# The first block of a row-sum kernel loaded as two partition halves from two issuing engines

## The chip, the core and the metric

The kernel runs on one core of a Trainium2 chip. A core has several engines that work side by side and meet only through semaphores. Those that matter here are VectorE (DVE in the profile), ScalarE (ACT), GpSimd (POOL) and SyncE (SP; its instructions that issue transfers are listed as SPq). Sixteen DMA engines move data between the chip's memory (HBM) and the core's working memory (SBUF), which has 128 partitions. The metric is the device time of one execution in microseconds; less is better.

## The reference

The input is 32 × 512 rows of 1024 float32 numbers, 67.1 MB. The output is one float32 for each row: the sum of its positive entries.

```python
def setup_inputs():
    batch, seq, dim = 32, 512, 1024
    return {"x": np.random.randn(batch, seq, dim).astype(np.float32)}

def reference(x: np.ndarray) -> np.ndarray:
    relu_x = np.maximum(x, 0)
    return np.sum(relu_x, axis=-1).astype(np.float32)
```

There is one clamp and one addition for each number read, and 64 KB of output.

## The kernel before

The 16,384 rows are taken as eight blocks of 2,048 rows. A block is 128 partitions × 16 rows × 1024 numbers: 64 KB in each partition and 8.39 MB in all. The first block is the first 2,048 rows of the input, 16 neighbouring rows to a partition (`xf`, line 83); the others are cut from the rest of the input (`xv`, line 84). Three SBUF buffers `io0` to `io2` of one block each are used in turn (line 74).

The loop of lines 183 to 203 goes over seven blocks. For each, SyncE issues one transfer for the whole block (the helper `load`, lines 101 to 108; the issue is line 103 in the profile). Each load has a semaphore of its own, which the transfer raises by 16 when it has landed. From the fourth block on, the load first waits until VectorE has finished with the block that was in its buffer three blocks ago (`freed`, lines 104, 105 and 185). SyncE does nothing but issue transfers and wait, in program order.

The work on a block is split by `TWO` (line 14): ScalarE clamps a run of rows in place (`clamp`, activation in line 144), and VectorE sums the clamped run (`total`, tensor_reduce in line 152). The first two blocks are one run of 16 rows each, the next ones two runs of 8. Some rows at the end are done whole by one engine, clamp and sum in one instruction: ScalarE in line 159 and VectorE in line 167. Before its first clamp ScalarE loads its table of functions (line 142), and that instruction carries the wait for the first block.

The eighth block is cut into loads that become smaller (lines 206 to 244: 8 rows, 4 rows, and four pieces of the last 4 rows), so that little work is left when the last bytes land. GpSimd clamps one small piece (line 234), VectorE folds the last piece in (line 254), and SyncE stores the sums in three transfers (line 115).

The order on the queues is written out by hand; nothing is planned by a tool. `open_without_barrier` (lines 268 to 284) edits the program's opening: it takes out the barrier and moves the first load (`EARLY = 1`) ahead of everything else that SyncE does, so that the first load is SyncE's first instruction. At the end, `tile_relu_sum_kernel` clears the semaphores (lines 47 to 50). All transfers are issued by SyncE, on one queue.

## Time and profile before

| what | value |
|---|---|
| device time, median of 3 runs | 161.03 us (160.95 to 161.07) |
| span of the profiled execution, first to last instruction | 159.7 us |
| the profiled execution's own time | its span is all that the profile gives; the median of the runs is 1.3 us above it |
| DVE busy | 118.8 us (74% of the span) |
| ACT busy | 103.6 us (65%) |
| DMA moved | 67.18 MB, mean 421 GB/s, 98.0% of 16 engines' span |
| first block landed | 22.0 us after the start of the span |
| second block landed | 41.3 us |

The page of the profile lists busy time by engine, then the span in 40 equal slices of about 4 us each, the DMA queues, the chain of work that ended last, the costliest groups of instructions, and the transfers that were issued. Times are in microseconds from the first instruction, which is the first block's load. A DMA packet is one contiguous piece that one DMA engine moves: for a whole block it is one partition's 64 KB, so a block is 128 packets.

### The profile page before, as it was taken

Reading aid. Unit: us, or ns where it says so; the run is one execution under the profiler, and the core shown is the slowest. Engines: PE = TensorE matmul, PEld = TensorE weight load, DVE = VectorE, ACT = ScalarE, POOL = GpSimd, SP = SyncE. Lnnn points to the kernel's source line nnn. Section 1 sums busy time; section 2 is a strip of 40 time slices with the busy share of each in tenths; the row PEclk is TensorE's granted clock in tenths of the full one; section 3 lists DMA queues with packets and bytes.
Section 4 is the critical chain, followed back from the end, with each engine's and each line's share of the span. In section 5 each row is a group of like instructions: output and inputs, shape, how many; then the busy total and the mean of one; then the engine's idle time right before and its main releaser. Section 6 shows DMA issues by size and latency. Waiting matters only on the chain.

```text
span 159.7 us, 125 instructions
## 1 busy us (share of the span) xinstructions
DVE 118.8 (74%) x44; ACT 103.6 (65%) x53; POOL 1.0 (1%) x5
## 2 busy tenths in 40 slices
DVE  0000000006999799999999999999999799999986
ACT  0000049993699808996099951999329993496995
POOL 0000000000000000000000000000000000000001
DMA  7996996996997997979969969969969969898993
GB/s 263 525 525 263 525 509 279 525 509 279 525 476 312 525 443 345 525 328 460 525 279 509 525 263 525 525 263 525 509 279 525 492 295 525 353 435 386 407 409 128
DMA packets 2304, 67.18 MB, mean 421 GB/s; under 512 B 640, under 2 KB 768, under 8 KB 1024
## 3 DMA queue, kind: packets, MB, share of 16 engines
q1 hardware_dynamic: 2304, 67.18, 98.0%
HBM read 67.11 MB, written 0.07 MB: 421 GB/s over the span
## 4 chain that ended last, share of the span: by engine, by line
DVE 45%; DMA 45%; ACT 9%; SPq 1%; issue 0%
DMA io<-in_x_dram 45%; DVE res L152 43%; ACT io L144 9%; DVE io L167 1%; SPq L103 1%; DVE io L126 1%; DVE io L254 0%
## 5 line engine op out<-in xcount | busy, mean ns | idle before, releaser
L152 DVE TENSOR_REDUCE res<-io 128x8 f32<-128x8192 f32 (+2 forms) x10 | 101.1, 10175 | 38.9 <-ACT io L144 38.9
L144 ACT ACTIVATE io<-io 128x8192 f32<-128x8192 f32 (+2 forms) x10 | 81.8, 8218 | 25.9 <-DMA io<-in_x_dram 25.9
L159 ACT ACTIVATE io<-io 128x1024 f32<-128x1024 f32 x18 | 18.8, 1043 | 6.6 <-DMA io<-in_x_dram 6.6
L167 DVE TENSOR_SCALAR_CACHE_REDUCE io<-io 128x1024 f32<-128x1024 f32 x14 | 16.2, 1214 | 0.5 <-DMA io<-in_x_dram 0.4
L142 ACT ACT_TABLE_LOAD x1 | 1.3, 1283 | 22.0 <-DMA io<-in_x_dram 22.0
L159 ACT ACTIVATION_READ_ACCUMULATOR io<-io 128x1 f32 x18 | 3.4, 187 | 0.0
L234 POOL TENSOR_SCALAR io<-io 128x254 f32<-128x254 f32 x1 | 0.8, 840 | 155.1 <-DMA io<-in_x_dram 155.1
L167 DVE DVE_READ_ACCUMULATOR io<-io 128x1 f32 x14 | 1.1, 82 | 0.0
L126 DVE TENSOR_SCALAR_CACHE_REDUCE io<-io 128x552 f32<-128x552 f32 (+1 forms) x2 | 1.1, 596 | 0.0
L121 ACT ACTIVATE io<-io 128x321 f32<-128x321 f32 (+1 forms) x2 | 0.9, 426 | 0.1
L254 DVE SCALAR_TENSOR_TENSOR io<-last,io 128x254 f32<-128x254 f32 x1 | 0.4, 425 | 0.0
L121 ACT ACTIVATION_READ_ACCUMULATOR io<-io 128x1 f32 x2 | 0.4, 187 | 0.0
L121 ACT ACTIVATE last<-last 128x153 f32<-128x153 f32 x1 | 0.3, 332 | 0.0
L121 ACT ACTIVATION_READ_ACCUMULATOR last<-last 128x1 f32 x1 | 0.2, 187 | 0.0
L126 DVE DVE_READ_ACCUMULATOR io<-io 128x1 f32 x2 | 0.2, 84 | 0.0
L299 POOL MEMSET const-bfloat16-1.0<- 128x1 bf16 x1 | 0.1, 101 | 0.0
L299 POOL MEMSET const-uint8-127<- 128x1 uint8 x1 | 0.1, 101 | 0.0
L299 POOL MEMSET const-float32-0.0<- 128x1 f32 x1 | 0.1, 99 | 0.2 <-issue 0.2
L299 POOL MEMSET const-float32-1.0<- 128x1 f32 x1 | 0.1, 98 | 0.0
L254 DVE DVE_READ_ACCUMULATOR io<-last,io 128x1 f32 x1 | 0.1, 83 | 0.0
## 6 DMA issues: line engine op xcount, KB each, us to landing
io<-in_x_dram SPq DMA_DIRECT2D x1, 4096.0 KB, 23.8
io<-in_x_dram SPq DMA_DIRECT2D x1, 2048.0 KB, 28.3
io<-in_x_dram SPq DMA_DIRECT2D x1, 1151.0 KB, 30.6
io<-in_x_dram SPq DMA_DIRECT2D x1, 436.5 KB, 31.2
io<-in_x_dram SPq DMA_DIRECT2D x1, 259.0 KB, 31.4
last<-in_x_dram SPq DMA_DIRECT2D x1, 201.5 KB, 31.4
io<-in_x_dram SPq DMA_DIRECT2D x7, 29.1
out_dram<-res SPq DMA_DIRECT2D x1, 55.0 KB, 1.6
```

The source lines that it names most:

```text
L103: dma = nc.sync.dma_start(out=dst, in_=src)
L121: nc.scalar.activation(out=ap, in_=ap, func=RELU, accum_out=accum_out).wait_op(*after, "sem-ge").then_inc(sems.end, 1)
L126: i = nc.vector.tensor_scalar(out=ap, in0=ap, scalar1=0.0, scalar2=None, op0=MAX, op1=ADD, accum_out=accum_out,)
L142: nc.scalar.preload_act_table(RELU).wait_op(loaded, 16, "sem-ge")
L144: i = nc.scalar.activation(out=ap, in_=ap, func=RELU)
L152: nc.vector.tensor_reduce(out=res[:, m : m + n], in_=ap, axis=mybir.AxisListType.X, op=ADD).wait_op(sems.act, n_act, "sem-ge").then_inc(se ...
L159: i = nc.scalar.activation(out=ap, in_=ap, func=RELU, accum_out=accum_out)
L167: i = nc.vector.tensor_scalar(out=ap, in0=ap, scalar1=0.0, scalar2=None, op0=MAX, op1=ADD, accum_out=accum_out,)
L234: nc.gpsimd.tensor_scalar(out=clamped, in0=clamped, scalar1=0.0, scalar2=None, op0=MAX).wait_op(loaded, 16, "sem-ge").then_inc(sems.end, 1)
L254: nc.vector.scalar_tensor_tensor(out=clamped, in0=last[:, : 2 + LAST_DVE], scalar=0.0, in1=clamped, op0=MAX, op1=ADD, accum_out=res[:, NT ...
L299: nc = _bacc.Bacc("TRN2", target_bir_lowering=False, num_devices=1)
```

## The change

The first block is no longer one transfer. SyncE loads partitions 0 to 63, and ScalarE issues a transfer of its own for partitions 64 to 127. Every partition still gets its 64 KB as one contiguous piece. ScalarE's transfer raises a new semaphore, `half`; ScalarE waits for it before its table load, which itself still waits for SyncE's half. VectorE's first sum waits for ScalarE's clamp, as before. `open_without_barrier` now moves ScalarE's first instruction to the head of its stream as well, so each of the two engines begins with its half of the load. All other loads stay as they were.

```diff
@@ tile_relu_sum_kernel
-    nums = sorted(s.num for s in (*sems.loads, sems.act, sems.dve))
+    nums = sorted(s.num for s in (*sems.loads, sems.act, sems.dve, sems.half))
@@ Semaphores
         self.dve = tc.alloc_semaphore("dve")
+        self.half = tc.alloc_semaphore("half")
@@ relu_sum
-        loaded = load(buf[:, :, :], rows(m, ROWS), j >= NBUF and freed[j - NBUF])
+        if j == 0:
+            H = P // 2
+            loaded = load(buf[:H, :, :], rows(m, ROWS)[:H])
+            nc.scalar.dma_start(out=buf[H:, :, :], in_=rows(m, ROWS)[H:]).then_inc(
+                sems.half, 16
+            )
+            nc.scalar.wait_ge(sems.half, 16)
+        else:
+            loaded = load(buf[:, :, :], rows(m, ROWS), j >= NBUF and freed[j - NBUF])
@@ open_without_barrier
-    SP = mybir.EngineType.SP
...
-    loads = [i for i in body if i.engine == SP][:n_loads]
-    for i in loads:
-        assert isinstance(i, mybir.InstDMACopy)
-        body.remove(i)
-    at = next(n for n, i in enumerate(opening) if i.engine == SP)
-    opening[at:at] = loads
+    for engine in (mybir.EngineType.SP, mybir.EngineType.Activation):
+        loads = [i for i in body if i.engine == engine][:n_loads]
+        for i in loads:
+            assert isinstance(i, mybir.InstDMACopy)
+            body.remove(i)
+        at = next(n for n, i in enumerate(opening) if i.engine == engine)
+        opening[at:at] = loads
```

## The prediction

> **What bounds the kernel now.** I read the 40 slices of the page first, then a table of stretches cut at the landings, then the timeline, the queue's own waits, and last a close look at the first 10 us.

> ```profile
> DMA  7996996996997997979969969969969969898993
> GB/s 263 525 525 263 525 509 279 525 509 279 525 476 312 525 443 345 525 328 460 525 279 509 525 263 525 525 263 525 509 279 525 492 295 525 353 435 386 407 409 128
> q1 hardware_dynamic: 2304, 67.18, 98.0%
> ```

> The DMA engines are busy 98.0% of the span. The odd 263 and 525 are packets booked whole: 16 packets of 64 KB in a 4 us slice are 263 GB/s, 32 are 525. So the sixteen engines move one packet each at the same time, in rounds.

> ```profile
> 4.00:22.00 18.00, 0.00 (x0) 0.01 (x1) 0.00 (x0) 1.00 1.08 466
> 22.00:41.30 19.30, 4.13 (x1) 15.13 (x2) 0.00 (x0) 1.00 1.00 435
> 41.30:60.70 19.40, 18.59 (x2) 13.89 (x2) 0.00 (x0) 1.00 1.00 432
> 60.70:80.00 19.30, 19.30 (x2) 13.92 (x2) 0.00 (x0) 1.00 1.00 435
> 80.00:99.40 19.40, 19.40 (x4) 13.97 (x3) 0.00 (x0) 1.00 1.00 432
> ```

> The last two columns are the DMA share and GB/s. Between landings the DMA share is 1.00 and the rate 432 to 435 GB/s: transfer-bound. A block is 128 packets, 8 rounds.

> ```profile
> 21.99 1.28 ACT L142 ACT_TABLE_LOAD   x1 [21.99 <-DMA io<-in_x_dram]
> 23.29 13.86 ACT L144 ACTIVATE io<-io 128x16384 f32<-128x16384 f32 x1
> 37.17 17.22 DVE L152 TENSOR_REDUCE res<-io 128x16 f32<-128x16384 f32 x1 [37.17 <-ACT io L144]
> 41.32 13.86 ACT L144 ACTIVATE io<-io 128x16384 f32<-128x16384 f32 x1 [4.18 <-DMA io<-in_x_dram]
> 55.21 17.22 DVE L152 TENSOR_REDUCE res<-io 128x16 f32<-128x16384 f32 x1 [0.81 <-ACT io L144]
> ...
> 60.67 13.95 ACT L144 ACTIVATE io<-io 128x8192 f32<-128x8192 f32 x2 [5.49 <-DMA io<-in_x_dram]
> 72.46 53.84 SPq L103 DMA_DIRECT2D io<-in_x_dram  x8
> 80.03 13.95 ACT L144 ACTIVATE io<-io 128x8192 f32<-128x8192 f32 x2 [5.42 <-DMA io<-in_x_dram]
> ```

> ScalarE waits for each landing: 21.99, 41.32, 60.67, 80.03. The spacing is 19.35 us, 2.42 us a round. VectorE frees the first buffer at 37.17 + 17.22 = 54.4, and the fourth load is issued at 54.75 (a timeline row of the queue), 5.9 us before the queue would run dry at 60.67; the fifth is issued at 72.46, 7.6 us ahead of 80.03. So the queue never waits for VectorE, and the end is the start of the transfers, plus their time, plus a short tail.

> ```profile
> SPq L103 <- DVE res L152: 121.3, 5, 53.1
> ```

> SyncE's 121.3 us of waiting for VectorE is therefore no loss: five loads that are issued early enough. The first block is the only one that pays a start: it lands at 21.99, 2.64 us more than 19.35. The close look shows where, in slices of 0.25 us, where one packet is 262 GB/s:

> ```profile
> GB/s 0 0 0 0 2621 1311 0 0 262 0 0 0 0 0 0 0 2097 1835 262 0 0 0 0 0 0 0 3146 786 262 0 0 0 0 0 0 262 3146 524 262 0
> ```

> Ten packets start at 1.0 us, five at 1.25, one at 2.0; the second round starts at 4.0 to 4.75, and the next two from 6.5 and 8.75. Nothing moves for 1.0 us after the issue; the first round takes 3 us in place of 2.42. In every round 15 of 16 packets start within about 0.5 us.

> **The change part by part.** The sum is made against the span of 159.7 and carried to the median, 161.03: the 1.33 us between them is what lies around the span, and I leave it as it is.

> SyncE: one issue before, one after. Its row in line 103 is 0.33 to 0.47 us; half the partitions may shorten the first one, by at most that, and the second load follows in a queue that is full for 20 us. Nothing to count.

> ScalarE: one issue (bounded by the same row, at most 0.47 us) and one wait, both before its table load. Behind the wait stand the table load, the clamp of line 144, and through it VectorE's first sum. ScalarE is idle until 21.99 anyway, so both cost nothing; without that cover the issue would cost 0.47. When the first block lands, ScalarE still has 4.18 us of slack before the second block, and the table load's 1.28 stays where it was.

> Semaphores: SyncE's clear spans one more, still one instruction at the end. Nothing.

> The transfer: the same 128 packets of 64 KB, but now 64 in one queue and 64 in another, each set going to only half the partitions. This is the whole of the case, and the trace of before has no load on fewer than 128 partitions and no second queue, so it has to be bounded. Lower bound: the two queues feed the engines together and the start shortens. The 1.0 us to the first packet is paid by either queue; what can go is the rest of the start, 2.64 - 1.0 = 1.6 us. Upper bound: a partition takes data no faster than any load of the trace shows. That is 432 GB/s over 128 partitions, 3.4 GB/s each, so 64 partitions take 216 GB/s. If all sixteen engines, in rounds as the rows show, start with SyncE's half and then all turn to ScalarE's, each of the 8 rounds of the block takes 4.84 us in place of 2.42: +19.36 us.

> Between -1.6 and +19.36 I stand near the upper end, since the nearest rows are those that show the engines in step: 15 of 16 start within 0.5 us of a 2.42 us round, so at nearly all times they would all be on the same half. What being slightly out of step saves: if two engines that write the same group of partitions are a lag L apart, a round takes 4.84 - L for both, and 8 rounds save 8 L. The pair with the least lag sets the landing. Sixteen starts in 0.5 us are 0.03 apart on average, so L is 0 to 0.25 (half the spread). I take 0.07 for the closest pair, a saving of 0.56.

> Sum: 161.03 + 19.36 - 0.56 = 179.8 us. After the first block everything is a rigid shift: the loads that follow have all 128 partitions again, the fourth load's 5.9 us of slack moves along with its buffer, and no later stretch has spare DMA time to win anything back.

> [...]

> **The rivals.**
> Out of step (163.4 us, or anything up to 177). If of two engines on the same partitions one is served first, it finishes its packet in 2.42 us and turns to the other half, and from then on half of the engines write one half and half the other. The loss is one round, +2.42. The same comes about if the second queue reaches some of the engines first. For it: one engine of the first round starts 1 us after the others. Against it: the other 15 are in step.

> No cost (161.0 us). If each half is moved by eight engines of its own, 8 packets each, the traffic is that of before. For it: 64 packets divide into 8 rounds of 8 as well as into 4 rounds of 16. Against it: every load in the trace keeps all sixteen engines busy, and its semaphore rises by 16, which this change asks for in both halves too.

> Faster (160.5 us). Two queues, each with half as many packets to hand out, bring the engines to work sooner. Its place is the first 4 us: the first round's 0.6 us above 2.42 and the straggler at 2.0. Taking 0.5 us as a third of the 1.6 at stake gives 160.5. It decides only if both halves together run at 432 GB/s, so that the first block lands before 21.99. For it: the DMA engines have no other idle time than start and tail, and every microsecond there counts in full. Against it: 10 of 16 packets start in one slice of 0.25 us already, so handing out is not slow. [...]

> **How the numbers follow.** Half rate through the first block: 0.70, 179.8 us, its own range 177.4 (a lag of 0.25) to 181.0 (no lag, and the second issue standing behind the first for 0.47). Out of step: 0.12, 163.4 to 177. No cost: 0.06, within 0.2% (0.3 us, about what a measurement of this kernel can tell). Faster: 0.12, 160.5. Slower is 0.70 + 0.12 = 0.82. A range from 163.0 to 181.0 holds the first two, 0.82, and leaves out the last two.

> **What would show it.** The table load of line 142 begins at about 40.8 in place of 21.99; rates near 216 GB/s in the stretch up to there; then landings 19.35 us apart as before, at about 60, 79.5 and 99. The fourth load would still be issued some 5.9 us before it is needed. A first landing at 24.4 means out of step; at 22.0, no cost; below, faster. The prediction is wrong if the rate of a load does not depend on how many partitions are written at one time, or if the engines fall out of step at once.

## The result, and the profile after

The changed kernel takes 181.53 us (median of 4 runs, 181.35 to 181.64) against 160.99 us for the kernel before on the same chip: a ratio of 1.128, interval 1.126 to 1.129. It is slower by 20.5 us. The forecast was 179.8 us with a range of 163 to 181, so the direction was right, the forecast was 1.7 us too low, and the range was missed by 0.5 us.

The page of the changed kernel, with the span, the 40 slices (4.5 us each now) and the two queues:

```profile
span 179.9 us, 127 instructions
DMA  9999999569999799999979999997899999699994
GB/s 233 233 233 233 233 233 219 117 146 452 466 466 437 306 423 466 466 466 466 437 321 408 466 466 466 466 452 335 379 466 466 466 466 452 291 423 466 386 397 164
q1 hardware_dynamic: 2240, 62.98, 87.1%
q10 hardware_dynamic: 80, 4.19, 11.0%
```

The first six slices hold 16 packets each (233 GB/s), the later ones mostly 32 (466); a packet is booked whole in the slice in which it starts. The DMA engines are as busy as before all the while: busy is not fast. ScalarE's half is the 4.19 MB of q10. How that looks after the start is in the table of stretches (length, busy time of DVE, ACT and POOL, clock, DMA share, GB/s):

```profile
5.00:10.00 5.00, 0.00 (x0) 0.00 (x0) 0.00 (x0) 1.00 0.99 210
10.00:20.00 10.00, 0.00 (x0) 0.00 (x0) 0.00 (x0) 1.00 0.99 210
20.00:30.00 10.00, 0.00 (x0) 0.00 (x0) 0.00 (x0) 1.00 0.99 210
...
61.40:80.80 19.40, 18.98 (x2) 13.86 (x1) 0.00 (x0) 1.00 1.00 432
80.80:100.20 19.40, 19.40 (x2) 13.95 (x2) 0.00 (x0) 1.00 1.00 432
```

210 GB/s as long as the first block is on its way, 432 from then on, as before. And the timeline, start and duration first:

```profile
0.12 0.55 ACTq L189 DMA_DIRECT2D io<-in_x_dram  x1
42.58 1.28 ACT L143 ACT_TABLE_LOAD   x1 [42.58 <-DMA io<-in_x_dram]
57.76 17.22 DVE L153 TENSOR_REDUCE res<-io 128x16 f32<-128x16384 f32 x1 [57.76 <-ACT io L145]
61.51 13.86 ACT L145 ACTIVATE io<-io 128x16384 f32<-128x16384 f32 x1 [3.79 <-DMA io<-in_x_dram]
...
80.87 13.95 ACT L145 ACTIVATE io<-io 128x8192 f32<-128x8192 f32 x2 [5.50 <-DMA io<-in_x_dram]
```

The first block lands at 42.58 in place of 21.99, 20.6 us late. The second lands at 61.51 (41.32 before), the third at 80.87 (60.67): 20.2 us late each. The whole loss is in the first block, and the rest is the kernel before, moved to the right. The queue does not run dry: the fourth load is issued when VectorE is done with the first block, 57.76 + 17.22 = 75.0, which is 5.9 us before 80.87. In the kernel before it was 37.17 + 17.22 = 54.4, which is 6.3 us before 60.67.

### The profile page after: what moved, and what is told of

It is laid out like the page before. It is cut to its first block, busy times and chain, and to the rows that moved or that the text cites. A ratio compares the mean times of both kernels' runs of the same rounds, so it can differ in the third digit from the quotient of the medians.

```text
span 179.9 us, 127 instructions
## 1 busy us (share of the span) xinstructions
DVE 118.8 (66%) x44; ACT 103.6 (58%) x53; POOL 1.0 (1%) x5
## 2 busy tenths in 40 slices
DMA packets 2320, 67.18 MB, mean 373 GB/s; under 512 B 656, under 2 KB 784, under 8 KB 1040
## 3 DMA queue, kind: packets, MB, share of 16 engines
q10 hardware_dynamic: 80, 4.19, 11.0%
## 4 chain that ended last, share of the span: by engine, by line
DMA 41%; DVE 40%; ACT 16%; another core or an unknown queue 2%; SPq 0%; issue 0%; ACTq 0%
DMA io<-in_x_dram 41%; DVE res L153 38%; ACT io L145 15%; ACT L143 1%; DVE io L168 1%; DVE io L127 1%; SPq L104 0%; DVE io L263 0%; ACTq L192 0%
## 5 line engine op out<-in xcount | busy, mean ns | idle before, releaser
L160 ACT ACTIVATE io<-io 128x1024 f32<-128x1024 f32 x18 | 18.8, 1043 | 6.6 <-DMA io<-in_x_dram 6.6
```

The source lines that it names most:

```text
L160: i = nc.scalar.activation(out=ap, in_=ap, func=RELU, accum_out=accum_out)
```

## The experiments

Twelve kernels were run, each beside the kernel before (160.9 to 161.0 us in all of them). Each changes only the way in which the first block is loaded and what goes with it, and all of them move the same bytes unless said otherwise. Where one queue does it all, only SyncE's first load is moved to the head of its stream. The trace's packet records have queue, start, time and size of each packet, but not its engine; two packets are taken to be of one engine where the second starts as the first ends.

| run | first block as | time, us | against before (interval) |
|---|---|---|---|
| the change | two halves, two queues | 181.53 | 1.128 (1.126 to 1.129) |
| one_queue | two halves, one queue | 182.51 | 1.134 (1.132 to 1.136) |
| rows_split | rows 0-7 and 8-15, two queues | 161.40 | 1.0027 (1.0017 to 1.0037) |
| source_spread | two halves, other source rows | 181.35 | 1.127 (1.124 to 1.129) |
| quarters | four times 32 partitions | 182.11 | 1.131 (1.129 to 1.134) |
| middle | 32-95, 0-31, 96-127 | 172.06 | 1.069 (1.066 to 1.072) |
| even_odd | even and odd partitions, two queues | 161.62 | 1.004 (1.002 to 1.006) |
| sixteens | eight times 16 neighbours | 216.56 | 1.346 (1.342 to 1.350) |
| staggered | the change and a small transfer more | 193.95 | 1.205 (1.199 to 1.212) |
| stripes | every 4th of a half, halves in turn | 181.25 | 1.126 (1.123 to 1.129) |
| stripes_pad | an extra transfer, then stripes | 180.96 | 1.124 (1.111 to 1.137) |
| step8 | every 8th partition | 182.42 | 1.133 (1.130 to 1.137) |
| out_of_step | stripes, extra transfer behind the first | 169.68 | 1.055 (1.049 to 1.060) |

### Is it the second queue, the source or the partitions?

Three causes could halve the rate: the engines' going to and fro between two queues, the narrower source in HBM, and the partitions written. One run for each.

**one_queue** keeps the halves and drops the second queue.

```diff
-            nc.scalar.dma_start(out=buf[H:, :, :], in_=rows(m, ROWS)[H:]).then_inc(
+            nc.sync.dma_start(out=buf[H:, :, :], in_=rows(m, ROWS)[H:]).then_inc(
                 sems.half, 16
             )
```

> Both halves of the first block are issued by SyncE, one behind the other on one queue; ScalarE issues nothing. Theory P (the rate depends on which partitions are being written at the same time): each half has the engines on 64 partitions only, so its 4 rounds take 4.94 us each as in the changed kernel, first landing near 42, time about 181.5 us. Theory Q (an engine that alternates between two queues loses time at each change): one queue, no alternation, rounds of 2.42 us, first landing near 22, time about 161.

Measured 182.51 us. The first block lands later still:

```profile
43.31 1.28 ACT L143 ACT_TABLE_LOAD   x1 [43.31 <-DMA io<-in_x_dram]
```

Theory Q falls: no second queue, and the loss is there. The packet records of the trace give 5.12 us for a packet whose engine stays on the half (4.93 where it crosses to the other), against 4.93 to 4.97 in the changed kernel, where it crosses at every packet.

**rows_split** keeps the second queue and drops the halves.

```diff
-            H = P // 2
-            loaded = load(buf[:H, :, :], rows(m, ROWS)[:H])
-            nc.scalar.dma_start(out=buf[H:, :, :], in_=rows(m, ROWS)[H:]).then_inc(
+            H = ROWS // 2
+            loaded = load(buf[:, :H, :], rows(m, H))
+            nc.scalar.dma_start(out=buf[:, H:, :], in_=rows(m + H, H)).then_inc(
                 sems.half, 16
             )
```

> The two queues stay, but each moves all 128 partitions: SyncE rows 0 to 7 of each partition, ScalarE rows 8 to 15, in packets of 32 KB (half of the 64 KB, so 16 rounds for the block). Theory P: all partitions are written in every round, so the block moves at 432 GB/s and the time is 161.0, give or take the 0.5 us of a changed start. Theory Q: 16 changes of queue in place of 8; at 2.5 us lost at each that is 200 us, and if the loss goes with the bytes, 181.5.

Measured 161.40 us, 0.27% above before. In the table of stretches of this run the rate stays full through the first block, and the timeline has the first landing at 22.38:

```profile
10.00:20.00 10.00, 0.00 (x0) 0.00 (x0) 0.00 (x0) 1.00 0.99 429
```
```profile
22.38 1.28 ACT L143 ACT_TABLE_LOAD   x1 [22.38 <-DMA io<-in_x_dram]
```

Two queues cost 0.4 us at the first landing (22.38 against 21.99), 0.2 us at the second (41.49 against 41.32), and no rate. This is also the fair trial of the rival "faster": two queues that start together at full rate, and the first block lands later, not sooner.

**source_spread** lets each half read from all over the 8.39 MB. The sums of the first block then go out in two stores in place of one, which the lines below leave out.

```diff
+            spread = x_flat[:N1].rearrange("(p t m) d -> t p m d", p=H, t=2)
-            loaded = load(buf[:H, :, :], rows(m, ROWS)[:H])
-            nc.scalar.dma_start(out=buf[H:, :, :], in_=rows(m, ROWS)[H:]).then_inc(
+            loaded = load(buf[:H, :, :], spread[0])
+            nc.scalar.dma_start(out=buf[H:, :, :], in_=spread[1]).then_inc(
                 sems.half, 16
             )
...
```

> As the changed kernel, but each half reads every second 64 KB of the first 8.39 MB of the input, so both halves read all over the 8.39 MB; the partitions written are the same, and the sums of the first block are stored with two transfers to match. Theory P: 181.5 us, packets as in the changed kernel. Theory S (the halves are slow because each reads from only 4.2 MB of HBM at a time): near 161.

Measured 181.35 us, with 210 GB/s through the first block again:

```profile
10.00:20.00 10.00, 0.00 (x0) 0.00 (x0) 0.00 (x0) 1.00 0.99 210
```

The source is not it. What is left is the set of partitions that is written at a time.

### Their number, or which ones?

**quarters** and **sixteens** make the sets smaller. The edit shown is that of quarters; sixteens has `P // 8`, `range(1, 8)` and a wait for 7 × 16.

```diff
+            Q = P // 4
+            loaded = load(buf[:Q, :, :], rows(m, ROWS)[:Q])
+            for q in range(1, 4):
+                nc.sync.dma_start(
+                    out=buf[q * Q : (q + 1) * Q, :, :],
+                    in_=rows(m, ROWS)[q * Q : (q + 1) * Q],
+                ).then_inc(sems.half, 16)
+            nc.scalar.wait_ge(sems.half, 48)
```

> The first block in four transfers of 32 partitions each (0 to 31, 32 to 63, 64 to 95, 96 to 127), one behind the other on SyncE's queue. Theory P1 (a partition takes 3.3 GB/s at most, so the rate falls with the number of partitions written): 32 partitions take 105 GB/s, the block 80 us in place of 20, time about 221. Theory P2 (partitions share their way in, and 32 neighbouring ones reach as much of it as 64): the block takes as long as in halves, time about 181.5. Theory Q: 161. [...]

> The first block in eight transfers of 16 neighbouring partitions on SyncE's queue. [...] Theory F (any transfer on fewer than 128 partitions runs at 210 GB/s, whatever the number, as 64 and 32 did): about 182.

Measured 182.11 and 216.56 us. 32 partitions go as fast as 64. With 16 a round of sixteen packets takes 9.35 us by the packet records, against 5.12 with 32. The stretches, of quarters and then of sixteens:

```profile
20.00:30.00 10.00, 0.00 (x0) 0.00 (x0) 0.00 (x0) 1.00 1.00 210
```
```profile
20.00:30.00 10.00, 0.00 (x0) 0.00 (x0) 0.00 (x0) 1.00 0.94 105
```

The 105 is one round booked in 10 us; 16 packets of 64 KB in 9.35 us are 112 GB/s.

With 210 GB/s into 32 partitions a partition takes 6.6 GB/s, nearly twice the 3.4 that the prediction had as its bound. So there is no bound of 3.4 GB/s to a partition, and theory P1 falls. Nor does F hold, since 16 partitions are slower than 32.

**middle** takes 64 partitions again, but others: 32 to 95. By the rates so far, 32 to 63 add nothing to 0 to 31 (210 GB/s in quarters and in one_queue), and the whole 128 take twice as much (432). Theory G is one grouping that would give these rates.

```diff
+            loaded = load(buf[32:96, :, :], rows(m, ROWS)[32:96])
+            for lo in (0, 96):
+                nc.sync.dma_start(
+                    out=buf[lo : lo + 32, :, :], in_=rows(m, ROWS)[lo : lo + 32]
+                ).then_inc(sems.half, 16)
+            nc.scalar.wait_ge(sems.half, 32)
```

> The first block in three transfers on SyncE's queue: partitions 32 to 95, then 0 to 31, then 96 to 127. The first is 64 partitions again, but from both halves. Theory N (the number of partitions written at a time sets the rate, 64 or fewer run at 210 GB/s): all 8 rounds take about 5 us, time about 182, as in halves. Theory G (partitions share a way in by groups, p and p + 32 the same one, and p + 64 another): the first transfer reaches all the ways, its 4 rounds take 2.42 us; the other two reach half of them, 4 rounds of 5.1; the block lands near 32.5, time about 171.7. [...]

Measured 172.06 us (theory G: 171.7). One transfer of 64 partitions runs at full rate (2.42 us for a packet from the second round on, as in the kernel before), and its two smaller followers at half rate (5.0 to 5.1 us from their second round on):

```profile
2.00:12.00 10.00, 0.00 (x0) 0.00 (x0) 0.00 (x0) 1.00 1.17 426
...
20.00:30.00 10.00, 0.00 (x0) 0.00 (x0) 0.00 (x0) 1.00 1.01 210
```

**even_odd** and **step8** take sets that lie all over the 128.

```diff
+            loaded = load(buf[0:P:2, :, :], rows(m, ROWS)[0:P:2])
+            nc.scalar.dma_start(out=buf[1:P:2, :, :], in_=rows(m, ROWS)[1:P:2]).then_inc(
+                sems.half, 16
+            )
```
```diff
+            sets = [slice(o, o + 121, 8) for o in range(8)]
+            for ps in sets:
+                nc.sync.dma_start(out=buf[ps, :, :], in_=rows(m, ROWS)[ps]).then_inc(
+                    loaded if ps is sets[-1] else sems.half, 16
+                )
```

> Two queues as in the changed kernel, SyncE takes the even partitions and ScalarE the odd ones, 64 each, spread over all 128. Theory H (what counts is that both the lower and the upper 64 are written at a time): full rate, about 161. [...]

> The first block in eight transfers of 16 partitions on SyncE's queue, every eighth partition (0, 8, ... 120), then 1, 9, ..., up to 7, 15, .... [...]

even_odd took 161.62 us, full rate; step8 took 182.42, half rate, although its 16 partitions lie all over the 128. The first landings, of even_odd and then of step8:

```profile
22.44 1.28 ACT L143 ACT_TABLE_LOAD   x1 [22.44 <-DMA io<-in_x_dram]
```
```profile
43.32 1.28 ACT L143 ACT_TABLE_LOAD   x1 [43.32 <-DMA io<-in_x_dram]
```

A transfer of step8 has 16 packets, and I take it that each of the sixteen engines gets one of them, so that partitions 0, 8, ... 120 are written at the same time; no record has a packet's engine. In even_odd a transfer has 64 packets, four for each engine if they are shared out evenly, and I had assumed that an engine gets four that follow one another. The engines would then stand on 0, 8, ... 120 at the same time, and even_odd would have been as slow as step8 (182.42 us). It was not (161.62), so the assumption is wrong; how a transfer's partitions are dealt to the engines when each gets several was not settled, nor why the sets of step8 are slow. Theory H, that both halves being written is enough, is wrong by step8.

### Do the engines slow each other, or is each slow by itself?

The prediction's rival was that engines which are out of step would lose next to nothing. To put them out of step, eight of the engines get one packet more than the others. Four runs; only the last settles it.

**staggered** adds a small transfer to ScalarE's queue.

```diff
+            nc.scalar.dma_start(
+                out=bufs[2][H : H + 32 : 4, :4, :], in_=rows(0, 4)[H : H + 32 : 4]
+            ).then_inc(sems.pad, 16)
             nc.scalar.dma_start(out=buf[H:, :, :], in_=rows(m, ROWS)[H:]).then_inc(
...
+            if j == 2:
+                nc.sync.wait_ge(sems.pad, 16)
```

> The changed kernel with one small transfer more: ScalarE first loads 8 packets of 16 KB (the first 4 rows of partitions 64, 68, ... 92, into the third buffer, where the third block overwrites them), then its half; SyncE waits for that small transfer before it issues the third block. Eight partitions go to eight of the engines, and delay these by one small packet, so that they take the halves in the opposite order to the other eight. Theory O (out of step, as in the prediction's rival: the loss is only that all sixteen engines stand on the same half, and if eight stand on the other there is none): one round of 4.9 us, one small packet, then rounds near 2.45; the first block lands near 25, time about 164.5. Theory E (a load on half the partitions is slow in each engine, whatever the others do): about 182.

Measured 193.95 us, worse than either theory had it. In the packet records the small packets moved eight engines by 1.2 to 1.5 us. In three of the rounds that followed (from about 12, 27 and 32 us) eight engines took from one queue and eight from the other, so that eight were on each half, and packets still took 5.0 to 5.3 us. Either an engine is slow by itself, or engines that slow each other were both among the eight; since it is not known how the partitions of these transfers are dealt to the engines, the run can't say. It cost more for another reason. ScalarE's half came last on some engines, and the first block landed at 57.84; VectorE freed its buffer only at 90.2, after the third block had landed (89.24) and the queue had run dry:

```profile
57.84 1.28 ACT L144 ACT_TABLE_LOAD   x1 [57.84 <-DMA io<-in_x_dram]
...
89.24 13.95 ACT L146 ACTIVATE io<-io 128x8192 f32<-128x8192 f32 x2 [2.50 <-DMA io<-in_x_dram]
```
```profile
84.00:91.20 7.20, 7.20 (x2) 4.70 (x2) 0.00 (x0) 1.00 0.34 146
```

A DMA share of 0.34: the slack of about 6 us that the fourth load has in the kernel before and in the changed one was used up here, since the first block came 35.9 us later than in the kernel before and the third only 28.6.

**stripes** and **stripes_pad** do it on one queue, one transfer behind the other, with transfers of 16 partitions, one for each engine as I take it, so that all the packets of a round go to one half. The first edit is that of both; stripes_pad has the second one ahead of the loop, and the wait before the third block as in staggered.

```diff
+            sets = [slice(h + o, h + o + 61, 4) for o in range(4) for h in (0, 64)]
+            for ps in sets:
+                nc.sync.dma_start(out=buf[ps, :, :], in_=rows(m, ROWS)[ps]).then_inc(
+                    loaded if ps is sets[-1] else sems.half, 16
+                )
```
```diff
+            nc.sync.dma_start(
+                out=bufs[2][64:93:4, :, :], in_=rows(0, ROWS)[64:93:4]
+            ).then_inc(sems.pad, 16)
```

> Control for the next one. The first block in eight transfers of 16 partitions on SyncE's queue, every fourth partition of one half (0, 4, ... 60), then of the other (64, 68, ... 124), and so on with 1, 65, 2, 66, 3, 67. [...] All theories by which halves are slow: rounds of 4.94 us, time about 182.

> The same eight transfers, with one of 8 packets of 64 KB ahead of them (partitions 64, 68, ... 92 of the third buffer, overwritten later by the third block). It gives eight engines one packet more than the others, so that these stand on one half while the other eight stand on the other half, in every round. Theory O (two engines that want the same way in share it; an engine alone on it has all of it): rounds of 2.42 us, the extra packet costs one of them, time about 164. Theory E (a transfer of a half is slow in each engine by itself): rounds of 4.94, time about 184 to 187. The same would come if the two that share a way in are both among the eight that are delayed.

stripes took 181.25 us, as foretold, with packets of 4.92 us. stripes_pad took 180.96. The extra transfer was meant to part the engines, but its issue took 0.80 us and the other eight started 2.1 us later, which nearly undid it. Starts and durations of packets from the trace's records, one engine with the extra packet and one without:

```
with:     1.56 (3.23)  4.79 (4.41)  9.20 (4.68)  13.88 (4.63)  18.51 (4.58) us
without:  3.75 (4.29)  8.03 (4.67)  12.71 (4.64)  17.35 (4.59)  21.94 (4.57) us
```

The two sets of eight engines stay about 1 us apart, and a packet takes 4.6 in place of 4.92 us. Two readings come of it. The extra packets, which eight engines wrote into the upper half with nobody else there, took 2.7 to 3.3 us, and the first packets of the kernel before 2.4 to 3.3: eight packets into eight partitions of one half (64, 68, ... 92) are not slow. And a lag of about 1 us saved 0.3 us a round.

**out_of_step** puts the extra transfer behind the first of the eight.

```diff
             for ps in sets:
...
+                if ps is sets[0]:
+                    nc.sync.dma_start(
+                        out=bufs[2][0:29:4, :, :], in_=rows(0, ROWS)[0:29:4]
+                    ).then_inc(sems.pad, 16)
```

> The eight transfers of every fourth partition once more, with the extra transfer of 8 packets of 64 KB (partitions 0, 4, ... 28 of the third buffer, overwritten later) put behind the first of them in place of ahead of it. Ahead of it, the eight engines without an extra packet started 2.1 us after the others (first packets at 3.7 to 4.1 us against 1.55 to 1.73), so all sixteen stood on the same half again, 0.9 us apart; that run told nothing. Now the sixteen engines share the first round, then eight do the extra packet while the other eight go on to the other half, and from there on eight stand on each half in every round. Theory O (two engines that want the same way in share it, one alone has all of it): one round of 4.9 us, then rounds of 2.42, one packet more on eight engines; first block near 26, time about 165. Theory E (a transfer of a half is slow in each engine by itself): rounds of 4.9, time about 184 to 186.

Measured 169.68 us, 11.6 less than stripes, with 0.5 MB more to move. The stretches:

```profile
5.00:10.00 5.00, 0.00 (x0) 0.00 (x0) 0.00 (x0) 1.00 1.12 419
10.00:15.00 5.00, 0.00 (x0) 0.00 (x0) 0.00 (x0) 1.00 1.07 419
15.00:20.00 5.00, 0.00 (x0) 0.00 (x0) 0.00 (x0) 1.00 0.78 301
20.00:25.00 5.00, 0.00 (x0) 0.00 (x0) 0.00 (x0) 1.00 1.08 393
25.00:30.00 5.00, 0.00 (x0) 0.00 (x0) 0.00 (x0) 1.00 1.06 288
```

Packets are booked whole where they start, so single stretches jump; from 5 to 25 us the mean is 383 GB/s, against 210 in stripes. The same transfers to the same partitions run at nine tenths of the full rate once eight engines stand on one half and eight on the other. So theory E falls: a transfer of a half is not slow by itself, the engines slow each other when all of them want the same half. That leaves the other reading of staggered, which no record shows: where eight engines on each half were slow (5.0 to 5.3 us a packet), engines that slow each other were both among the eight. The 169.68 is above the 165 foretold because packets took 2.5 to 2.8 us (2.7 to 3.3 in the second round) and because at the end, from 25 us, the eight late engines and the first packets of the second block met again (4.6 to 5.0 us by the records).

## Why the prediction was right in kind and too low by 1.7 us

**What bounds the kernel** was read rightly: the queue never waits for VectorE, so what the first block's load loses is the loss of the kernel. 20.2 us of lateness are passed on unchanged from the second landing to the end. The fourth load was issued 6.3 us before it was needed in the kernel before, and 5.9 us in the changed one. (The prediction has 5.9 for the kernel before: its 54.75 is the end of that issue, which began at 54.4.)

**The edits costed at nothing** cost nothing: ScalarE's issue, 0.55 us and so longer than the 0.47 it was bounded by, and its wait lie ahead of a table load that begins at 42.58, and 3.79 us of ScalarE's slack before the second block are left.

**The transfer.** The sum was 19.36 - 0.56 = +18.8, eight rounds of 4.84 - 0.07 = 4.77 us in place of 2.42; the span grew by 20.2. A round was 4.94 us in the packet records of the changed kernel, 212 GB/s and not 216. That is 8 × 0.17 = 1.4 us more, and 18.8 + 1.4 = 20.2.

- The step that failed is the one that called 3.4 GB/s a partition, and with it an even split of 4.84 us a round, the upper bound of the cost. Sharing cost 2% more than an even split in the changed kernel (4.94 us) and 6% more where engines do not change halves (5.12 us in one_queue). And a partition has no such bound: 32 partitions took the rate of 64 (210 GB/s, quarters), and another 64 took twice that rate (426, middle). By the prediction's own last sentence it is wrong here, since the rate does not go with the number of partitions written. That the figure came out nearly right is luck: half of the partitions had half the rate here (210 of 432 GB/s), but so had a quarter of them, for which the same bound would have been far off (221 us expected by it in quarters, 182.11 measured).
- That sixteen engines stand on one half together and share what it takes was right, as out_of_step shows (383 GB/s with eight engines on each half, 210 in stripes with all of them on one).
- The lag between engines, -0.56 us or 0.07 a round, can't be told apart from this. Against 4.84 nothing was saved. Against the 5.12 us of a packet whose engine stays on its half, one that crosses took 0.19 us less (4.93 in one_queue), and in stripes_pad two sets of engines about 1 us apart took 0.3 us less than stripes. So a gain of the lag's direction is there, but which two engines slow each other, and so their lag, is in no record, and that the lag makes the gain is not shown. The engines start their second packets at 5.60 to 6.98 us, and the earliest as well as the latest keep their places from there on:

```
earliest:  1.33 (4.28)  5.60 (4.97)  10.55 (4.95)  15.49 (4.95)  20.42 (4.94) us
latest:    1.55 (5.43)  6.98 (4.93)  11.90 (4.93)  16.83 (4.93)  21.76 (4.93) us
```

Three small terms that the sum does not have cancel each other, by the means over the sixteen engines. The first packets start 0.2 us later. The first round, 0.6 us longer than the others in the kernel before, has no such excess here (4.86 us). And the second block's first packets take 2.9 us in place of 2.42. The median grew by 0.3 us more than the span: each execution of the changed kernel took 1.6 us more than its span, and the kernel before 1.3 to 1.4; what that is the profile does not say. In the close look at the first 10 us of the changed kernel (slices of 0.25 us, one packet 262 GB/s) the first packets start at 1.25 in place of 1.0:

```profile
GB/s 0 0 0 0 0 3146 786 0 262 0 0 0 0 0 0 0 0 0 0 0 0 0 262 262 1311 1049 1049 262 0 0 0 0 0 0 0 0 0 0 0 0
```

one_queue's first issue takes 0.55 us too, while quarters' takes 0.39 and rows_split's ScalarE issue 0.37, so this goes with the partitions of the transfer and not with the second queue. It is not their number alone: the stepped sets of 16 in stripes and step8 took 0.58 us, the 16 neighbours of sixteens 0.39.

**The range** ended at 181.0 because half rate was taken for the worst that sharing can do, with an issue's 0.47 us on top. It should have had room for sharing that costs more than an even split. The lower end of that outcome's own range was also added up wrongly: 161.03 + 19.36 - 8 × 0.25 is 178.4 and not 177.4, which changes nothing here.

**The rivals.** "Faster" had its trial in rows_split and did not come. "No cost" needed eight engines for each half; in the first 10 us of the changed kernel the sixteen engines write 16 packets of SyncE's half and then 16 of ScalarE's. "Out of step" exists (out_of_step, where an extra transfer makes it), but it did not come about by itself in the change: a spread of 1.4 us between engines did not grow into it in eight rounds. Which engines slow each other within the two halves of the change was not found out.

## What to carry to other kernels

The rate of the loads here depended on which partitions the sixteen DMA engines were writing at the same moment, so measure for any split by partitions what rate each piece gets: 0 to 63 took 210 GB/s, but 32 to 95 took 426 and all 128 took 432. Split a load along the rows of each partition if it has to be split (0.27% here), and count a DMA engine's busy share only together with its GB/s, since both kernels show it at 0.99 to 1.00 while one moves half as much. In this transfer-bound kernel a loss at the head was paid in full at the end (20.2 us at the second landing and in the span).

## What was not expected

- Packets of 64 KB, with all sixteen engines on one half, take 5.12 us when the engine stays on that half and 4.93 to 4.97 when it crosses (one_queue, the change). Twice the 2.42 us of the kernel before is 4.84, which is less than either. With 16 neighbours a round took 9.35 us, and four times 2.42 is 9.68, which is more. Why the two differ stays open.
- Being out of step by a little saves much less than the lag: about 1 us apart saved 0.3 us a round (stripes_pad), while a full packet apart brought 383 GB/s back (out_of_step). Why the gain is not in proportion stays open.
- The first issue of the changed kernel's 64 partitions takes 0.55 us against 0.38 us in the kernel before, and its first packets start 0.3 us later.
